# Second-set stores on ScalarE's DMA queue, and the prompt's output weights loaded 13 and used 15 steps later

## The chip, the cores and the metric

The kernel runs on one core of a Trainium2 chip. The metric is the device time of one execution in microseconds (us); less is better. The time before is 2841.52 us, the median of three runs (2840.78 to 2841.62).

The core's engines run side by side, each through its own list of instructions in order: TensorE (PE in the profile; PEld is its weight loads), VectorE (DVE), ScalarE (ACT), GpSimd (POOL), and SyncE (SP), which here only issues DMAs. DMAs can also be issued by ACT; in this kernel q1 is SP's hardware queue and q10 ACT's. An instruction at an engine's head that has to wait holds up all that stands behind it on that engine, and this holds for an issue of a DMA as for a computation.

## The reference

One inference step of two layers, on 256 prompt tokens and 2048 sample tokens (a grid of 32 rows by 64 columns), with a width of 1024 and 16 heads of 64. Layer 0 is a convolution branch, layer 1 neighbourhood attention. Each is `x = x + gate * Mixer(RMSNorm(x) * (1 + scale) + shift)`. Cut to what the change touches:

```python
q, k, v, z = na_project(h, w_in)                 # h @ w_in, 1024 -> 4 x 1024
# prompt tokens: softmax over the 256 prompt tokens
out = (context_attention(q, k, v) * silu(z)) @ w_out
# sample tokens: softmax over 8 x 16 neighbours on the grid and 512 cached context keys
att = neighbourhood_attention(q, k, v, cache_k, cache_v, rpb)
out = (att * silu(z)) @ w_out
x = x + gate * out
y = rms_norm(x, final_g)
```

All inputs and outputs are 32-bit floats. The kernel multiplies with full precision kept by splitting numbers into a rounded high part and the rest (`h` and `l` at the end of names), with three products per matmul of two split operands.

## The kernel before, in words

**First phase.** The convolution layer is followed by the projection into keys (part 1), queries (part 0), values and gates (part 3, `z`) of layer 1. Tokens go through it in two sets: the first has the prompt and the first 768 sample tokens, the second the sample tokens from 768 to 2047, in three blocks of 512, 512 and 256. For the second set, `na_rest` loops over 8 column tiles of 128 (two heads each), over the three parts, and over the three blocks: 24 matmuls into a PSUM bank, then an evacuation. A gate block is evacuated by ACT's Silu (L1005) and stored to the DRAM tensor `zn_d` (L1006); a key block is rounded by ACT (L1101), its rest made by POOL or DVE, and both parts are stored per head by `store_keys` (L1110, L1111) to `ks_d`; a query block is stored by `store_q` (L1076, L1082) to `qh_d` and `ql_d`. `store_keys` is also called by `context_keys`, for the cached keys (`kc_d`). The evacuated blocks are tiles of the pool tag `st` with 6 buffers, so a block's buffer comes free when its store is done. Beside the second set, woven in, run the context keys, the masked bias, the gated output weights (`w2_d`), the prompt's attention (which leaves its gated output in `yp_d`) and the context values. All these DMAs, loads and stores, are on SP's queue. In this phase of the second set a scheduler fixes the order on every engine.

**Second phase, `attention()`.** 256 units: 16 heads in two halves (`hg` 0 and 1), 4 groups `G` of 8 grid rows, 4 column blocks. A head here is one head in one row group, so 4 units. The order is half 0, groups 0 to 3 with 8 heads each, then half 1. In step i, PE's list has the transposes of unit i−2, the values of unit i−3 in every second step, and the scores of unit i+1 at the end. `load_head` asks for a head's keys, bias, queries (2 buffers), gates and values one head ahead. PE and DVE are ordered by hand in this phase; ACT, POOL and SP by the scheduler.

The output projection is done by `out_group` in side chunks of 6 matmuls, one in each step without values, and one more in every fourth step while more than 16 are due. `out_group` goes over 128-token row tiles and two halves `h` of 512 columns (12 matmuls each, L1644 to L1646), with the bank evacuated in a later step by ACT (`evacuate`, L1668) and added to the residual `x` by POOL (L1669). The residual tile is loaded (L1627) into one of 3 buffers. Its two weight tiles per half (a high and a low part, 1 MB each) come from `load_w2` (L1600), into 4 buffers, so that one pair (`hg`, `g`) fills them; `g` is 0 for the prompt and 1 for the sample. The next pair's half is asked for when the last row tile's matmuls of that half have been issued, in the order (0, 0), (1, 0), (0, 1), (1, 1). For the first pair, `W2_STEP` sets the step; there `hold` writes one element of each tile on DVE first (L1599), so that the DMA can't be issued before DVE is at that step.

`BEGIN` is the step in which both halves of the prompt are put into the list of side work (with the loads of `yp` and a pause of 3 chunks). Before a row group's first output tile is made, `split` forces side chunks until no more than 7 row tiles are open, the new ones with them; this is the case first in unit 45, where group 0's tiles have been queued and group 1's are to be made.

Names: `o0_None_1_0` is the prompt's tile of half `hg` 0, row tile 1, column half 0; `o0_0_0_0` that of sample group 0. `w2h010` is the high part of the weights of `hg` 0, `g` 1, column half 0. `a0_6_qh` are the queries of group 0, head 6; `sa1_3_1_S` the scores of group 1, head 3, column block 1.

Of the kernel before, what the change touches and what calls it, by code (L numbers as in the profile page):

```python
# [11 lines left out]
F32 = mybir.dt.float32  # L12
# [33 lines left out]
ADA_LAG = 3.5  # L46
LEAD = 1.9
TMP = 4
BEGIN = 10
WAIT = 3  # L50
NEAR = 3
W2_STEP = 5
START = 45.0

W_START = {1: (0.55, 25.8, 26.6), 0: (26.0, 38.6, 39.5), 2: (36.0, 52.0, 52.6)}
# [21 lines left out]
class Kern:  # L77
    def __init__(self, ctx, tc, io):
        self.tc, self.nc, self.io = tc, tc.nc, io
        self.ctx = ctx  # L80
        self.cp = ctx.enter_context(tc.tile_pool(name="consts", bufs=1))
        self.dr = ctx.enter_context(tc.tile_pool(name="scratch", bufs=1, space=bass.MemoryType.DRAM))
        d = lambda name, shape: self.dr.tile(shape, F32, name=name, tag=name)
        self.zc_d = d("zc_d", [D, NTOK])
        self.wl_d = d("wl_d", [3 * NK, P, D])
        self.vc_d = d("vc_d", [D, VCOLS])
        self.x1_d = d("x1_d", [NTOK, D])
        self.qh_d = d("qh_d", [D, NTOK])
        self.ql_d = d("ql_d", [D, NTOK])
        self.ks_d = d("ks_d", [NH, 2, DH, NTOK])  # L90
        self.vp_d = d("vp_d", [NPR, NH, 2, DH])
        self.vs_d = d("vs_d", [GW // CW, NSA // GW, CW, NH, 2, DH])
        self.bm_d = d("bm_d", [NH, 3, P, 3, 480])
        self.zn_d = d("zn_d", [D, NTOK])
        self.kc_d = d("kc_d", [NH, 2, DH, NCTX])
        self.cvs_d = d("cvs_d", [NCTX, NH, 2, DH])
        self.w2_d = d("w2_d", [2, 2, D, D])
        self.x2_d = d("x2_d", [NTOK, D])
        self.gate_d = d("gate_d", [2, 2, D])
        self.rpb_d = d("rpb_d", [P + 1, RPB_PITCH])  # L100
        self.yp_d = d("yp_d", [NK, 2, P, NPR])
# [224 lines left out]
    def weight(self, w, c0, name):  # L326

        nc = self.nc
        return self.halves(w[:, c0 : c0 + P].rearrange("(k p) n -> p k n", p=P), [P, NK, P], name)
# [649 lines left out]
    def na_rest(self, blocks):  # L979

        nc, io = self.nc, self.io
        w_in = io["na_w_in"][0]
        order = lambda ct: (3, 1, 0) if ct == NK - 1 else (1, 0, 3)
        todo = [(ct, part) for ct in range(NK) for part in order(ct)]
        weight = lambda ct, part: self.weight(w_in, part * D + ct * P, f"ni{blocks[0][0]}{blocks[0][1]}_{ct}_{part}")
        ahead = weight(*todo.pop(0))
        yield
        for ct in range(NK):
            rows = slice(ct * P, ct * P + P)
            for part in order(ct):  # L990
                w = ahead
                if todo:
                    ahead = weight(*todo.pop(0))
                for src, t0, n, hi, lo in blocks:
                    nm = f"ni_{ct}_{part}_{src}{t0}"
                    pm = self.mm_bank(nm)[:, :n]
                    self.project(pm, w, (hi, lo))
                    a = self.col(src, t0)
                    if part == 1:
                        self.keys(ct, src, t0, n, pm, nm)  # L1000
                        continue
                    f = self.st(F32, nm + "_f", [P, n])
                    if part == 3:
                        with self.tc.high_priority():
                            nc.scalar.activation(f, pm, AF.Silu)  # L1005
                        nc.sync.dma_start(self.zn_d[rows, a : a + n], f)  # L1006
                        continue
                    fo, po = f, pm
                    if src == "s":
                        fo = f.rearrange("p (j r c) -> p r j c", j=4, c=16)  # L1010
                        po = pm.rearrange("p (r j c) -> p r j c", j=4, c=16)
                    with self.tc.high_priority():
                        nc.scalar.activation(fo, po, AF.Copy, scale=-(DH ** -0.5))
                    fh, fl = (self.st(F32R, f"{nm}_{s}", [P, n]) for s in ("h", "l"))
                    self.round_pool(fh, f)
                    self.rest_pool(fl, f, fh)
                    self.store_q(self.qh_d, rows, src, t0, n, fh.bitcast(F32))
                    self.store_q(self.ql_d, rows, src, t0, n, fl.bitcast(F32))
                yield
# [46 lines left out]
    def windows(raw, at, R):  # L1066

        ap = raw[:, at : at + 1]
        return bass.AP(ap.tensor, ap.offset, [ap.ap[0], [CW, 4], [BIAS_COLS, R], [1, CW]])

    def store_q(self, dst, rows, src, t0, n, f):

        nc = self.nc
        a = self.col(src, t0)
        if src == "p" or n == 512:
            nc.sync.dma_start(dst[rows, a : a + n], f)  # L1076
            return
        g0 = self.col(src, t0 // 512 * 512)
        r0 = t0 % 512 // GW
        nr = n // GW  # L1080
        d = dst[rows, g0 : g0 + 512].rearrange("p (j r c) -> p j (r c)", j=4, c=16)[:, :, r0 * 16 : (r0 + nr) * 16]
        nc.sync.dma_start(d, f.rearrange("p (j x) -> p j x", j=4))  # L1082

    def keys(self, ct, src, t0, n, pm, nm):

# [20 lines left out]
    def store_keys(self, dst, ct, a, n, kh, kl):  # L1106
        for i in range(2):
            h = 2 * ct + i
            sl = slice(i * DH, i * DH + DH)
            self.nc.sync.dma_start(dst[h, i, :, a : a + n], kh[sl, :].bitcast(F32))  # L1110
            self.nc.sync.dma_start(dst[h, 1 - i, :, a : a + n], kl[sl, :].bitcast(F32))  # L1111

    def context_keys(self):
        nc, io = self.nc, self.io
# [150 lines left out]
    def phase1(self):  # L1265
        tc = self.tc
        with ExitStack() as c:
# [30 lines left out]
                pass  # L1298
            late.close()
            norms.close()  # L1300
            rest = self.na_rest(B)
            with tc.tile_pool(name="bp", bufs=1, side="right") as self.bp:
                with tc.tile_pool(name="mb", bufs=1, side="right") as self.mb:
# [57 lines left out]
    def attention(self):  # L1361
# [10 lines left out]
        for i in range(-1, len(units) + 4):  # L1372
            self.step = i
            if i == W2_STEP:
                for h in range(2):
                    self.load_w2(0, 0, h, True)
            if i == BEGIN:
                for hg in range(2):
# [375 lines left out]
```

## Time and profile before

| | |
|---|---|
| time, median of 3 runs | 2841.52 us |
| the profiled execution's own time | 2847.02 us |
| its span | 2845.2 us |
| mean granted clock of PE | 0.981 |
| HBM read, written | 359.86 MB, 189.22 MB |

The profile is of one execution, which took 5.5 us more than the median; 1.8 us of its time lie outside the span. Times in its views count from the span's start. The second set runs from about 1360 to 1840 us, the second phase from there to the end. Busy shares are of the span; an engine that waits is not busy, and issuing DMAs is not counted as busy either.

### The profile page before, as it was taken

The page shows a single profiled execution, that of the slowest core. Times are in us where ns is not written, and L with a number is a line of the kernel's source. Part 1 is how long each engine was busy: PE and PEld are TensorE (multiplying, and loading weights), DVE is VectorE, ACT ScalarE, POOL GpSimd, SP SyncE. Part 2 cuts the span into 40 slices and gives each one's busy share as a digit, 9 for nine tenths or more (in the row PEclk, how much of TensorE's full clock was granted, in tenths as well). Part 3 has the DMA queues.
Part 4 walks back from the last instruction along what each step waited for, and adds up shares of the span by engine and source line. Part 5 has one row for each costly group of instructions (what it writes and reads, how often), then busy time and mean ns, then how long its engine had stood idle before and what let it go on. Part 6 is the DMA issues. An engine that isn't in the chain of part 4 may idle for free. (4 is left out here: it accounts for less than half of the span.)

```text
span 2845.2 us, 45399 instructions
## 1 busy us (share of the span) xinstructions
PE 2702.7 (95%) x16079; PEld 2339.1 (82%) x16079; DVE 1848.0 (65%) x3126; ACT 1448.6 (51%) x2544; POOL 1507.1 (53%) x1631
## 2 busy tenths in 40 slices
PE   6999999999899999999989999879999999999998
PEld 4888877777677888999988888768888898888887
DVE  4789989999886510023455632157787787777885
ACT  4457565667544311234222244246676666666774
POOL 4679878889653343355113325235555555455563
PEclk9999999999899999999999999999999999999999
DMA  7233554555445554447789996688876787866763
GB/s 254 68 121 117 185 187 158 179 177 187 154 120 164 165 156 130 131 141 229 240 285 347 346 307 194 185 247 221 245 206 190 200 216 181 239 184 178 199 168 105
DMA packets 435627, 548.02 MB, mean 193 GB/s; under 512 B 42945, under 2 KB 306201, under 8 KB 435272
## 3 DMA queue, kind: packets, MB, share of 16 engines
q1 hardware_dynamic: 430080, 522.17, 61.3%
q10 hardware_dynamic: 5320, 22.95, 2.1%
q8 instruction: 128, 2.10, 0.3%
q14 instruction: 99, 0.81, 0.1%
HBM read 359.86 MB, written 189.22 MB: 193 GB/s over the span
## 5 line engine op out<-in xcount | busy, mean ns | idle before, releaser
L1508 POOL TENSOR_SCALAR sa_p<-sa_p,sa_m 128x992 f32<-128x992 f32 (+2 forms) x256 | 278.6, 1088 | 445.7 <-DVE sa_m L1507 321.7
L502 DVE SCALAR_TENSOR_TENSOR cv<-u,dw,cv 128x640 f32<-128x640 f32 (+2 forms) x570 | 427.9, 822 | 3.7 <-ACT cv L498 2.8
L1523 ACT CAST sa_pt<-sa_T 128x512 fp32r<-128x512 f32 (+3 forms) x512 | 275.2, 588 | 235.0 <-PE sa_T L1514 230.6
L111 DVE TENSOR_TENSOR sa_pt<-sa_T,sa_pt 128x512 fp32r<-128x512 f32 (+3 forms) x512 | 328.4, 682 | 3.2 <-ACT sa_pt L1523 3.0
L351 PE MATMUL ci_ps<-h_s_hi,ci_wh 128*128 128x512 f32 x768 | 307.5, 400 | 2.0 <-DVE shift L239 1.0
L353 PE MATMUL ci_ps<-h_s_hi,ci_wl 128*128 128x512 f32 x768 | 303.2, 395 | 0.0
L352 PE MATMUL ci_ps<-h_s_lo,ci_wh 128*128 128x512 f32 x768 | 302.9, 394 | 0.0
L1500 DVE TENSOR_REDUCE sa_m<-sa_S 128x1 f32<-128x512 f32 x256 | 176.2, 688 | 184.2 <-PE sa_S L1482 169.7
L1506 ACT ACTIVATE sa_p<-sa_S,sa_m 128x992 f32<-128x992 f32 (+2 forms) x256 | 267.3, 1044 | 53.7 <-DVE sa_m L1502 42.4
L1514 PE MATMUL sa_T<-ident,sa_p 128*128 128x128 f32 (+3 forms) x2048 | 271.6, 275 | 8.1 <-DVE sa_pt L111 7.3
L1514 PEld LDWEIGHTS sa_T<-ident,sa_p 128*128 128x128 f32 (+3 forms) x2048 | 238.5, 138 | 42.5 <-issue 12.0
L480 ACT ACTIVATE cv_p<-u,dw 128x640 f32<-128x640 f32 (+2 forms) x326 | 241.4, 770 | 55.4 <-POOL cv_s L483 37.7
L483 POOL TENSOR_TENSOR cv_s<-cv_s,cv_p 128x519 f32<-128x519 f32 (+1 forms) x155 | 233.1, 1504 | 68.3 <-DVE cv_s L506 45.5
L483 POOL TENSOR_TENSOR cv_p<-cv_p,cv_p 128x520 f32<-128x520 f32 (+1 forms) x155 | 227.7, 1469 | 27.1 <-ACT cv_p L480 19.5
L1543 PE MATMUL sa_O<-sa_pt,a_v 120*128 120x256 f32 (+5 forms) x1280 | 192.5, 281 | 0.0
L1538 PE MATMUL sa_O<-sa_pt,cv 128*128 128x256 f32 x1024 | 176.3, 295 | 4.2 <-DVE 1_0_of L1557 1.7
L351 PEld LDWEIGHTS ci_ps<-h_s_hi,ci_wh 128*128 128x128 f32 x768 | 145.5, 189 | 39.3 <-ACT cv_p L480 2.5
L1502 DVE CUSTOM_DVE_ANT_0 sa_S<-sa_S,a_bm,sa_m 128x480 f32<-128x480 f32 (+2 forms) x256 | 170.9, 668 | 9.1
L353 PEld LDWEIGHTS ci_ps<-h_s_hi,ci_wl 128*128 128x128 f32 x768 | 145.1, 189 | 33.8
L352 PEld LDWEIGHTS ci_ps<-h_s_lo,ci_wh 128*128 128x128 f32 x768 | 145.6, 190 | 30.9
L1543 PEld LDWEIGHTS sa_O<-sa_pt,a_v 120*128 120x128 f32 (+2 forms) x1280 | 169.1, 193 | 0.0
L351 PE MATMUL ni_s<-h_s_hi,nis_wh 128*128 128x512 f32 x384 | 152.2, 396 | 12.4 <-DVE ni_s_l L111 8.7
(843 smaller groups left out, 7198.6 us busy)
## 6 DMA issues: line engine op xcount, KB each, us to landing
adaw<-in_ada_w SPq DMA_DIRECT2D x24, 1024.0 KB
ci_w<-in_conv_w_in SPq DMA_DIRECT2D x48, 512.0 KB
a_bm<-bm_d SPq DMA_DIRECT2D x32, 720.0 KB
x_s<-in_x_sample SPq DMA_DIRECT2D x32, 512.0 KB
vs_d<-v_s SPq DMA_DIRECT2D x128, 128.0 KB
a_qh<-qh_d SPq DMA_DIRECT2D x128, 128.0 KB
a_ql<-ql_d SPq DMA_DIRECT2D x128, 128.0 KB
o_x<-x_d SPq DMA_DIRECT2D x32, 512.0 KB
```

The source lines that it names most:

```text
L111: self.nc.vector.tensor_tensor(out=lo, in0=src, in1=hi.bitcast(F32), op=ALU.subtract)
L351: self.nc.tensor.matmul(out, wh[:, k, :], hh[:, k, :], start=k == 0, stop=False)
L352: self.nc.tensor.matmul(out, wh[:, k, :], hl[:, k, :], start=False, stop=False)
L353: self.nc.tensor.matmul(out, wl[:, k, :], hh[:, k, :], start=False, stop=k == NK - 1)
L480: nc.scalar.activation(t, st["u"][:, c0 + tap : c1 + tap], AF.Copy, scale=self.dw[:, ct, tap : tap + 1])
L483: nc.gpsimd.tensor_tensor(out=st["sum", half], in0=st["sum", half], in1=st[half, tap], op=ALU.add)
L502: nc.vector.scalar_tensor_tensor(out=out, in0=u, scalar=w, in1=first, op0=ALU.mult, op1=ALU.add)
L1506: nc.scalar.activation(p[:, n], S[:, n], AF.Exp, scale=-1.0, bias=m[:, 2:3], accum_out=m[:, 3:4])
L1508: nc.gpsimd.tensor_scalar(out=p[:, n], in0=p[:, n], scalar1=m[:, 3:4], scalar2=1.0, op0=ALU.mult, op1=ALU.mult)
L1514: nc.tensor.transpose(t[:w, c * P : c * P + P], p[:, x + c * w : x + c * w + w], self.ident)
L1523: nc.scalar.copy(pt[:w, 0, part, :, at], t)
L1543: nc.tensor.matmul(dst, v[:w, c0 + c].rearrange("p s d -> p (s d)"), loc[:, lo:hi], start=False, stop=s == 1 and c == 3)
```

## The change

Two numbers are raised: `BEGIN` from 10 to 25, and `W2_STEP` from 5 to 18. A flag `second` is set ahead of the second set's `na_rest`, and a helper `store` issues on ACT's queue while it is set, on SP's otherwise. The gate stores, `store_q` and `store_keys` go through it. That moves 200 DMAs to ACT's queue: 24 of gates, 48 of queries, 96 of keys and 32 of the cached keys. The stores of values, bias, gated weights and the prompt's attention stay on SP, as all loads do. Behind the flag lines count one to six more than before (L1005 is L1006, L1482 is L1488, L1600 is L1606, L1644 is L1650); the moved stores all have L1074.

```diff
@@ -46,10 +46,10 @@
 ADA_LAG = 3.5
 LEAD = 1.9
 TMP = 4
-BEGIN = 10
+BEGIN = 25
 WAIT = 3
 NEAR = 3
-W2_STEP = 5
+W2_STEP = 18
 START = 45.0
 
 W_START = {1: (0.55, 25.8, 26.6), 0: (26.0, 38.6, 39.5), 2: (36.0, 52.0, 52.6)}
@@ -78,6 +78,7 @@
     def __init__(self, ctx, tc, io):
         self.tc, self.nc, self.io = tc, tc.nc, io
         self.ctx = ctx
+        self.second = False
         self.cp = ctx.enter_context(tc.tile_pool(name="consts", bufs=1))
         self.dr = ctx.enter_context(tc.tile_pool(name="scratch", bufs=1, space=bass.MemoryType.DRAM))
         d = lambda name, shape: self.dr.tile(shape, F32, name=name, tag=name)
@@ -1003,7 +1004,7 @@
                     if part == 3:
                         with self.tc.high_priority():
                             nc.scalar.activation(f, pm, AF.Silu)
-                        nc.sync.dma_start(self.zn_d[rows, a : a + n], f)
+                        self.store(self.zn_d[rows, a : a + n], f)
                         continue
                     fo, po = f, pm
                     if src == "s":
@@ -1068,18 +1069,22 @@
         ap = raw[:, at : at + 1]
         return bass.AP(ap.tensor, ap.offset, [ap.ap[0], [CW, 4], [BIAS_COLS, R], [1, CW]])
 
+    def store(self, dst, src):
+
+        (self.nc.scalar if self.second else self.nc.sync).dma_start(dst, src)
+
     def store_q(self, dst, rows, src, t0, n, f):
 
         nc = self.nc
         a = self.col(src, t0)
         if src == "p" or n == 512:
-            nc.sync.dma_start(dst[rows, a : a + n], f)
+            self.store(dst[rows, a : a + n], f)
             return
         g0 = self.col(src, t0 // 512 * 512)
         r0 = t0 % 512 // GW
         nr = n // GW
         d = dst[rows, g0 : g0 + 512].rearrange("p (j r c) -> p j (r c)", j=4, c=16)[:, :, r0 * 16 : (r0 + nr) * 16]
-        nc.sync.dma_start(d, f.rearrange("p (j x) -> p j x", j=4))
+        self.store(d, f.rearrange("p (j x) -> p j x", j=4))
 
     def keys(self, ct, src, t0, n, pm, nm):
 
@@ -1107,8 +1112,8 @@
         for i in range(2):
             h = 2 * ct + i
             sl = slice(i * DH, i * DH + DH)
-            self.nc.sync.dma_start(dst[h, i, :, a : a + n], kh[sl, :].bitcast(F32))
-            self.nc.sync.dma_start(dst[h, 1 - i, :, a : a + n], kl[sl, :].bitcast(F32))
+            self.store(dst[h, i, :, a : a + n], kh[sl, :].bitcast(F32))
+            self.store(dst[h, 1 - i, :, a : a + n], kl[sl, :].bitcast(F32))
 
     def context_keys(self):
         nc, io = self.nc, self.io
@@ -1298,6 +1303,7 @@
                 pass
             late.close()
             norms.close()
+            self.second = True
             rest = self.na_rest(B)
             with tc.tile_pool(name="bp", bufs=1, side="right") as self.bp:
                 with tc.tile_pool(name="mb", bufs=1, side="right") as self.mb:
```

How it moves instructions is shown at three places. First, ACT's list at the end of the second set (the gates of a column tile, `ni_3`, and then its keys, `ni_1`; `pa` is the prompt's attention). Before:

```order
L1231 COPY pa_t<-pa_O 64x256
L1005 ACTIVATE ni_3_s_f<-ni_3_s_16991 128x512
L1005 ACTIVATE ni_3_s_f<-ni_3_s_17019 128x256
L1101 CAST ni_1_s_h<-ni_1_s_17053 128x512
L1101 CAST ni_1_s_h<-ni_1_s_17086 128x512
```

After:

```order
L1236 COPY pa_t<-pa_O 64x256
L1074 DMA zn_d<-ni_3_s_f 128x512
L1006 ACTIVATE ni_3_s_f<-ni_3_s_16991 128x512
L1074 DMA zn_d<-ni_3_s_f 128x512
L1006 ACTIVATE ni_3_s_f<-ni_3_s_17019 128x256
L1074 DMA zn_d<-ni_3_s_f 128x256
L1106 CAST ni_1_s_h<-ni_1_s_17053 128x512
L1074 DMA ks_d<-ni_1_s_h 64x512
L1074 DMA ks_d<-ni_1_s_l 64x512
```

The numbers in `ni_3` and `ni_1` are the parts. Each gate's store stands behind its Silu on ACT, and the store of a key's low part, which ACT doesn't make, stands ahead of ACT's next evacuation.

Second, SP's list around the prompt's first weights. Before:

```order
L1467 DMA ck7_18307<-kc_d_71 128x512
L1600 DMA w2h000_17397<-w2_d_73 128x4x512
L1600 DMA w2l000_17398<-w2_d_73 128x4x512
L1600 DMA w2h001_17403<-w2_d_73 128x4x512
L1600 DMA w2l001_17404<-w2_d_73 128x4x512
L1469 DMA cv7_18309<-cvs_d_72 128x4x128
L1477 DMA a0_3_v_17516<-vs_d_68 88x8x128
L1454 DMA a0_3_qh_17519<-qh_d_64 64x512
L1445 DMA a0_3_k_17514<-ks_d_66 128x704
```

After:

```order
L1460 DMA a0_5_ql_17853<-ql_d_65 64x512 x2
L1623 DMA yp0_1h_18292<-yp_d_77 128x4x128
L1623 DMA yp0_1l_18293<-yp_d_77 128x4x128
L1623 DMA yp1_0h_19039<-yp_d_77 128x4x128
L1623 DMA yp1_0l_19040<-yp_d_77 128x4x128
L1606 DMA w2h000_17944<-w2_d_73 128x4x512
L1606 DMA w2l000_17945<-w2_d_73 128x4x512
L1606 DMA w2h001_17950<-w2_d_73 128x4x512
L1606 DMA w2l001_17951<-w2_d_73 128x4x512
L1483 DMA a0_6_v_18027<-vs_d_68 88x8x128
L1460 DMA a0_6_qh_18030<-qh_d_64 64x512
L1451 DMA a0_6_k_18025<-ks_d_66 128x704
```

The four tiles stood ahead of head 3's loads, and stand ahead of head 6's, with four loads of `yp` ahead of them.

Third, PE's list in unit 45, where the matmuls that `split` forces reach the sample's first tile. Before:

```order
L1482 MATMUL sa1_3_1_S_19274<-a1_3_k_19030,a1_3_ql_19036 128x480
L1514 MATMUL sa1_2_3_T0_19279<-ident_98,sa1_2_3_p_19205 128x128 x4
L1514 MATMUL sa1_2_3_T1_19284<-ident_98,sa1_2_3_p_19205 120x128 x4
L1644 MATMUL o0_0_0_0_19304<-w2h010_18937,0_1_y0h_17811 128x512
L1645 MATMUL o0_0_0_0_19304<-w2l010_18938,0_1_y0h_17811 128x512
```

After:

```order
L1650 MATMUL o1_None_1_1_19266<-w2h101_19004,yp1_1h_19041 128x512
L1651 MATMUL o1_None_1_1_19266<-w2l101_19005,yp1_1h_19041 128x512
L1652 MATMUL o1_None_1_1_19266<-w2h101_19004,yp1_1l_19042 128x512
L1650 MATMUL o0_0_0_0_19290<-w2h010_19259,0_1_y0h_17749 128x512
L1651 MATMUL o0_0_0_0_19290<-w2l010_19260,0_1_y0h_17749 128x512
```

The prompt's second half stood in side chunks spread over the steps 27 to 40, and its four tiles now stand in unit 45, right ahead of the sample's first tile. That tile's weights, `w2h010` and `w2l010`, take the buffers which the prompt's second half reads. From unit 46 on, PE's list is the same in both.

## The prediction

> **What bounds the kernel now.** I read the page's busy times first, then windows to find the stages in which TensorE (PE) is not full, then PE's waits and the chain of waits in those.
>
> ```profile
> PE 2702.7 (95%) x16079; PEld 2339.1 (82%) x16079; DVE 1848.0 (65%) x3126; ACT 1448.6 (51%) x2544; POOL 1507.1 (53%) x1631
> q1 hardware_dynamic: 430080, 522.17, 61.3%
> q10 hardware_dynamic: 5320, 22.95, 2.1%
> ```
>
> PE is busy for 95% of 2845.2 us and nothing else is above 65%, so time is lost only where PE stands still or its granted clock falls. SP's queue is q1 with 522 MB, ACT's is q10 with 23 MB. The windows (us, PE, PEld, DVE, ACT, POOL, granted clock, DMA share, GB/s) show where:
>
> ```profile
> 1360.00:1520.00 160.00, 144.21 (x1016) 134.65 (x1015) 81.31 (x126) 36.58 (x68) 31.88 (x17) 0.97 0.84 273
> 1520.00:1800.00 280.00, 280.00 (x1547) 244.49 (x1546) 122.24 (x190) 100.29 (x207) 105.28 (x102) 1.00 0.84 279
> 1827.00:1831.00 4.00, 3.92 (x10) 3.16 (x11) 0.03 (x1) 0.60 (x1) 1.90 (x2) 0.56 0.58 145
> 1843.00:1873.00 30.00, 28.42 (x192) 24.74 (x192) 25.91 (x65) 21.76 (x41) 10.90 (x11) 0.94 1.05 338
> 1864.00:1873.00 9.00, 9.00 (x72) 8.59 (x70) 7.74 (x19) 6.17 (x13) 3.08 (x4) 1.00 1.04 385
> 1878.00:1891.00 13.00, 3.65 (x13) 2.98 (x14) 1.34 (x3) 0.59 (x1) 2.93 (x9) 0.51 1.03 207
> 1942.00:1948.00 6.00, 5.87 (x32) 5.66 (x33) 2.74 (x6) 2.14 (x4) 0.99 (x1) 0.72 1.05 244
> 1968.00:1978.00 10.00, 10.00 (x67) 8.94 (x66) 8.25 (x18) 6.42 (x12) 2.69 (x3) 1.00 0.83 225
> ```
>
> The second set begins at 1360 with 15.8 us of standing still, then PE is full from 1520 to 1800; the attention's start, behind that, stands repeatedly, and after each stand the clock is near half for some us. PE's waits from 1800 to 2035 (total, times, longest), and the chain there (start, us):
>
> ```profile
> PE sa_S L1481 <- DMA a_qh<-qh_d: 11.3, 1, 11.3
> PE sa_S L1482 <- DMA a_ql<-ql_d: 8.2, 4, 3.6
> PE ni_s L351 <- DVE ni_s_l L111: 7.1, 1, 7.1
> PE o_None L1644 <- ACT o_None_o L1668: 1.4, 2, 0.7
> ...
> 1818.51 7.53 DMA zn_d<-ni_s_f
> 1826.14 0.38 ACT ni_s_h L1101
> 1826.60 0.44 DVE ni_s_l L111
> 1827.08 0.80 PE ni_s L351
> 1861.77 15.76 DMA w2l<-w_d
> 1877.57 10.41 DMA a_ql<-ql_d
> 1888.11 0.77 PE sa_S L1482
> ```
>
> Two causes stand there. A gate store sits late on SP's queue, and the key evacuation behind it needs its buffer. And four 1 MB tiles of the prompt's output weights go ahead of a head's queries.
>
> **What it removes.**
>
> ```profile
> 1798.00 0.60 ACT L1005 ACTIVATE ni_s_f<-ni_s 128x512 f32<-128x512 f32 x1 [4.48 <-PE ni_s L353]
> 1884.52 0.76 PE L1481 MATMUL sa_S<-ck,a_qh 128*128 128x512 f32 x1 [11.29 <-DMA a_qh<-qh_d]
> ```
>
> (a) The gates were ready at 1798.6 and their store was issued at 1818.51: 19.9 us in SP's line. On ACT's queue it is issued at once and, with the same 7.53 in flight, lands near 1806, before PE needs the buffer at 1820. The 7.1 us wait goes, and the clock behind it (4 us at 0.56, so 1.8): **−8.9**.
> (b) W2(0,0) leaves the place ahead of head 3's loads. The 11.29 us stand goes, and the 2.8 behind it for the second query tile (from 1885.28 to 1888.11), and half clock over 3.65 us of work (1.8): **−15.9**.
> (c) Of the 8.2 us for ql tiles, 2.8 are already in (b). The other 5.4, at heads 5 and 6, come where out_group's loads crowd the queue; side work now starts 15 steps later, so I take them off with their clock (6 us at 0.72, 1.7): **−7.1**.
> The evacuation waits of o_None (1.4) recur, they are neither gained nor lost. Sum removed: 31.9.
>
> **What it adds.** The hold copies stood in step 5:
>
> ```profile
> L1599 DVE CAST w2h<-mhalf x2: 132/138/143, 1853.7 to 1853.8; 128x1 fp32r<-128x1 f32 x2
> 1843.28 0.99 POOL L1508 TENSOR_SCALAR sa_p<-sa_p,sa_m 128x864 f32<-128x864 f32 x1 [4.13 <-issue]
> ...
> 1871.66 0.99 POOL L1508 TENSOR_SCALAR sa_p<-sa_p,sa_m 128x864 f32<-128x864 f32 x1 [1.67 <-PE sa_O L1543]
> ```
>
> Ten steps without side work lie between the last two rows: 2.84 us each. From the hold at 1853.7 to the scores of head 3's first unit (1884.52 − 11.29 = 1873.23) are 19.5 us.
>
> (e) The hold at step 18 stands ahead of head 6, one step nearer: 16.7 us. A head is 1.79 MB of small pieces, at 207 to 225 GB/s (windows 1878 and 1968) 8.3 us. At the hold a backlog stands: head 5's 8.3, a gate tile 0.7 and four yp tiles 2.7 (1.31 MB at 385), 1.5 taken for flight, less three steps of 2.84 since head 5's buffers came free, so 4.7. Then W2's 4.19 MB at 385 GB/s (window 1864), 10.9, and head 6's 8.3: 23.9 against 16.7. PE stands 7.2 us, with clock 2.0: **+9.2**. Bounds: 0 if the backlog is gone and the queue runs at 385 throughout, 16 if it goes as at head 3 (b).
> (f) W2(1,0) now comes between steps 39 and 44, four tiles in five steps; 10.9 us of load against five steps of 2.84: **0**, up to 5 (half of the load) if a head's loads fall on it.
> (g) At unit 45 the split forces the prompt's last four tiles (48 matmuls) and two of the sample in a row, and W2(0,1) is used right behind the tiles whose buffers it needs. Twelve matmuls fill a tile's half:
>
> ```profile
> 1923.47 0.40 PE L1645 MATMUL o_None<-w2l,yp_1h 128*128 128x512 f32 x1
> 1924.61 0.40 PE L1481 MATMUL sa_S<-ck,a_qh 128*128 128x512 f32 x1
> ...
> 1797.80 0.28 PE L351 MATMUL ni_s<-h_s_hl,nis_wh 128*128 128x256 f32 x1
> 1800.62 0.39 PE L351 MATMUL ni_s<-h_s_hi,nis_wh 128*128 128x512 f32 x1
> ```
>
> Five of them lie between the first two starts, so 0.228 each and 2.74 for twelve (the 24 of 256 columns of a second-set group, between the last two, take 2.82). The first half (2.10 MB, 5.45 us at 385, 1.0 for flight) is asked for 2.74 before the burst's end: it lands 3.7 behind it, 0.7 of which an evacuation wait takes already (row o_None). The second half lands 5.45 later, while 12 matmuls and 0.7 pass: 2.1 more. 5.1, with clock 1.7: **+6.8**. Bounds 3 (the first half alone) and 17.5 (the 15.76 us that the last W2 tile took in the chain, with clock 1.7).
> (h) The residual x of o_0_1 waits for a prompt row's store, and its add now stands ahead of a POOL normalisation:
>
> ```profile
> SPq L1627 <- DMA x_d<-o_None_x: 5.2, 1, 5.2
> ```
>
> Nothing to 5.2; I take **+2**: nothing of PE's waits for x itself, only POOL's normalisation behind the add could.
> (i) Fifteen more steps have no side work to fill PE's short gaps; in the ten units without any (window 1843) PE stood 1.6 of 30 us, or 0.15 a unit, part of it at the start. I take 0.1 a step, **+1.5**, between 0 and 3. Sum added: 19.5.
>
> **The second set's line.** All 200 moved stores (30.4 MB) lie between 1360 and 1840.
>
> ```profile
> PE v_ps_s L973 <- DVE v_s L111: 6.5, 5, 2.3
> ACT v_s L1038 <- DMA vs_d<-v_s: 8.2, 4, 4.8
> ...
> L1110 SPq DMA_DIRECT2D kc_d<-ck_h x16: 484/580/1634, 1371.7 to 1399.6; - x16
> L1674 ACTq DMA_DIRECT2D x_d<-o_x x16: 326/326/333, 2031.8 to 2461.3; - x16
> ```
>
> The first two rows are waits from 1360 to 1520: value evacuations wait for their own stores, vs_d, which stay on SP but stood there behind 32 kc_d stores of 0.58 us each (18.6 us of issuing). These leave; the loads behind gain too. PE's 15.8 us there and 3% of clock (4.8) could at most go, 20.6; but DMA share is 0.84 already, so I take **−2.5**, near nothing, between −20 and +24. What is added is ACT's issuing: 200 × 0.33 to 0.58, 66 to 116 us in 480. ACT is busy 36% of 1520–1800, so it has room on average. A store also waits on ACT for what it stores. The low part is made by POOL after ACT, and what stands behind it on ACT is the next PSUM evacuation, which PE waits for two groups later:
>
> ```profile
> 1828.83 1.28 POOL L108 TENSOR_TENSOR ni_s_l<-ni_s_f,ni_s_h 128x512 fp32r<-128x512 f32 x1
> ```
>
> 1.28 and two issues (0.7) are 2.0, under the 2.82 us of a 256-column group, so it is hidden as long as POOL is on time; the cover gone, it is the slower rival below.
>
> **A rule against it.** The Trainium skill, "DMA: Bandwidth & Descriptors", section "Issuing engines are not separate DMA queues", says that DMAs of every issuer run on the same 16 engines and interleave, and that several issuers save only the sequencer's time, usually small. By it (a) would be nothing and the sum −6.0. The row 1818.51 speaks against it here: the store's flight was 7.53 us, its standing in line 19.9.
>
> **Sum.** −31.9 + 19.5 − 2.5 = **−14.9**. On the profiled execution's own time of 2847.02 that is 2832.1; this execution is 5.5 above the median 2841.52, and the difference taken from the median gives 2826.6, so 2827.
>
> **Rivals.**
> R1, the weights take their full price: term (g) is 17.5 instead of 6.8, −4.2 in all, 2837.3. For it: in the chain the last W2 tile took 15.76 us with heads beside it. Against: behind unit 45 fewer head loads stand in line. Chance 0.20.
> R2, the slower side: ACT's queue holds up evacuations where PE is full (1520–1800). It decides once POOL's low part comes over 0.8 us late (2.82 − 2.0). Price: about 1 us (a POOL normalisation or rest beside it is 0.99 to 1.28) for 3 blocks in 8 column tiles, 24. Then +9.1, 2850.6. For it: POOL has 105 us of side work there, unsplit. Against: 62% of POOL is free. Chance 0.17.
> R3, the stores land no sooner, because what they lack is the engines: (a) is gone, −6.0, 2835.5. For it: DMA share 0.84 around. Against: 19.9 against 7.53. Chance 0.05.
> R4, the second set's stands go by 15.8 instead of 2.5: −28.2, 2813.3. For it: its waits are for stores in SP's line; against: 273 GB/s is moved there, and the loads themselves remain. Chance 0.13.
> The forecast as it stands has 0.45.
>
> **How the numbers follow.** A measurement tells about 0.2% (5.7 us) from no change. Faster: forecast, R4 and most of R3, 0.61. Same: R1 and the rest, 0.22. Slower: R2, 0.17. For 8 in 10 the range goes from below R4 (with bounds of (e) and (c) the other way) at 2808 up to 2848, short of R2 at its full price.
>
> **What would show it.** After: ACT's queue near 53 MB; no 7 us wait of PE for ni_s's low part at 1820; head 3 on time and a wait of about 7 us for a_qh or a_ql at head 6; a PE wait of 3 and one of 2 us for w2h or w2l at unit 45; PE still full between 1520 and 1800. Wrong would be PE waits for ACT's evacuations there (R2), or a wait of over 10 us for the weights (R1); or a growth of the 15.8 us between 1360 and 1520 (the −2.5).

## The result and the profile after

The changed kernel takes 2854.08 us (median of 4 runs, 2851.91 to 2856.84), the one before 2841.15 us: a ratio of 1.0046, with a 95% interval of 1.0031 to 1.0060. 13 us are lost where 14.9 of gain were forecast, and the time lies outside the range.

The page of the changed kernel, its busy times and queues:

```profile
PE 2699.5 (95%) x16079; PEld 2332.0 (82%) x16079; DVE 1842.9 (65%) x3126; ACT 1448.3 (51%) x2544; POOL 1506.5 (53%) x1631
q1 hardware_dynamic: 403328, 491.75, 57.8%
q10 hardware_dynamic: 32072, 53.37, 5.5%
```

The 30.4 MB did move to ACT's queue, and no engine does more work. The windows (us, PE, PEld, DVE, ACT, POOL, granted clock, DMA share, GB/s):

```profile
1360.00:1520.00 160.00, 133.55 (x945) 125.44 (x946) 80.34 (x134) 33.77 (x64) 31.61 (x16) 0.95 0.88 283
1520.00:1800.00 280.00, 279.39 (x1541) 243.62 (x1540) 117.19 (x179) 101.87 (x207) 102.64 (x101) 1.00 0.81 267
```

From 1360 to 1520 PE is busy for 133.6 us; it was 144.2 before. Behind 1520 it is nearly full, as before. PE's waits there, and behind 1820 (total, times, longest):

```profile
PE v_ps_s L974 <- DVE v_s L112: 15.1, 11, 3.0
PE ni_s L352 <- DVE ni_s_l L112: 11.0, 1, 11.0
...
PE sa_S L1487 <- DMA a_qh<-qh_d: 5.8, 1, 5.8
PE sa_T L1520 <- DVE sa_pt L112: 5.0, 10, 1.5
PE ni_s L352 <- DVE ni_s_l L112: 3.8, 1, 3.8
PE sa_S L1488 <- DMA a_ql<-ql_d: 3.6, 2, 3.3
PE o L1650 <- DMA w2h<-w_d: 2.6, 1, 2.6
PE o L1651 <- DMA w2l<-w_d: 1.8, 1, 1.8
```

The second part is near the forecast: head 6's wait in place of head 3's, two waits for weights at unit 45. The first is not: the waits for the values' low parts have more than doubled, a stand of 11 us for a key block is new, and of the 7.1 us behind 1820, 3.8 are still there. From 1360 to 1520 PE's waits sum up to 26.5 us; they were 15.8. What held the key block stands in ACT's timeline (start, us, what, and the idle time before with its releaser):

```profile
1477.88 0.59 ACT L1106 CAST ni_s_h<-ni_s 128x512 fp32r<-128x512 f32 x1 [4.25 <-PE ni_s L354]
1481.31 0.62 ACT L1166 CAST w_100h<-w_100t 128x512 fp32r<-128x512 f32 x1 [2.83 <-DVE w_100t L1165]
1490.87 1.63 ACTq L1074 DMA_DIRECT2D ks_d<-ni_s_h  x2
1494.20 2.09 ACTq L1074 DMA_DIRECT2D ks_d<-ni_s_l  x2
1496.39 0.59 ACT L1106 CAST ni_s_h<-ni_s 128x512 fp32r<-128x512 f32 x1 [14.46 <-DMA bm_d<-bm]
```

ACT made the key's high part by 1478.47, and issued its store at 1490.87. Nothing of that store was missing: the tile was ready, and ACT had nothing else to do from 1481.93 on. ACT's next work, a key evacuation behind four stores, came after 14.46 us of idling. The row names a bias store (`bm_d`) as the releaser; that is the profile's inference, and this bias store landed only at 1497.95. The evacuation started 0.1 us behind the issue of the last of the four stores: it waited for the stores, and the question is what they waited for.

The built program shows why. It has eight completion counters (semaphores that a landing DMA increments) for the DMAs of SP and ACT together, given out in turn; in the trace, too, every DMA of the two counts on one of the same eight. Each DMA's issue waits until the DMA that had its counter last has landed, so at most eight are under way, and the line is one for both queues. ACT's list with its waits, there (DMAHW0 to DMAHW7 are the counters):

```
L1106 CAST ni_0_1_s1024_h_13812<-ni_0_1_s1024_13787 128x512 [waits DMAHW0_49,DMAHW7_49,PE_49,Activation_49]
L1166 CAST w2_100h_15586<-w2_100t_15585 128x512 [waits DMAHW6_49,DVE_49]
L1074 DMA ks_d_66<-ni_0_1_s1024_h_13812 64x512 [waits DMAHW6_49,Activation_49]
L1074 DMA ks_d_66<-ni_0_1_s1024_h_13812 64x512 [waits DMAHW0_49]
L1074 DMA ks_d_66<-ni_0_1_s1024_l_13813 64x512 [waits DMAHW2_49,DVE_49]
```

The second store reads what the first does and waits for a counter alone (DMAHW0). The trace has each counter's increments. The four stores stood 8.9, 0.7, 1.7 and 1.2 us, 12.5 of the 14.46, and each stand ended within 0.1 us of the last increment of the store's own counter, which had been given last to a DMA of SP: for the first, a bias store that SP had issued at 1485.15.

Over all 200 moved stores, 70 stood for over 0.3 us on ACT, 96.3 us in all. 44 of these (68.3 us) ended within 0.2 us of the last increment of the store's own counter, and for 35 (60.9 us) the DMA counted there was one of SP's. The other 26 (28.0 us) are not told apart here; low parts that come late are among the possible reasons. Not each of them costs PE time: 34.5 of the 96.3 us lie between 1543 and 1810, where PE stood 0.6 us in all.

### The profile page after: what moved, and what is told of

The parts are those of the page before. It is cut to its first block, busy times and chain, and to the rows that moved or that the text cites. A ratio compares the mean times of both kernels' runs of the same rounds, so it can differ in the third digit from the quotient of the medians.

```text
span 2850.1 us, 45331 instructions
## 1 busy us (share of the span) xinstructions
PE 2699.5 (95%) x16079; PEld 2332.0 (82%) x16079; DVE 1842.9 (65%) x3126; ACT 1448.3 (51%) x2544; POOL 1506.5 (53%) x1631
## 5 line engine op out<-in xcount | busy, mean ns | idle before, releaser
L484 POOL TENSOR_TENSOR cv_p<-cv_p,cv_p 128x520 f32<-128x520 f32 (+1 forms) x155 | 227.7, 1469 | 26.5 <-ACT cv_p L481 18.8
L109 POOL TENSOR_TENSOR nis_wl<-nis_w,nis_wh 128x1024 fp32r<-128x1024 f32 x24 | 58.8, 2454 | 227.5 <-ACT nis_wh L344 177.8
L352 PE MATMUL ni_s<-h_s_hi,nis_wh 128*128 128x512 f32 x384 | 152.0, 396 | 15.8 <-DVE ni_s_l L112 15.4
```

Of the source, the lines that this page charges most:

```text
L352: self.nc.tensor.matmul(out, wh[:, k, :], hh[:, k, :], start=k == 0, stop=False)
L484: nc.gpsimd.tensor_tensor(out=st["sum", half], in0=st["sum", half], in1=st[half, tap], op=ALU.add)
```

## The experiments

In the traces I compare the second set by three stretches of PE: A from the prompt's last value matmul to the second set's first `ni_s` matmul, B from there to the 301st, C to the 1701st (of 1728). Their bounds are starts in the timelines; in C, 290.1 is what the kernels without the wait at 1820 take. "Set" goes on to the first scores.

| kernel | A | B | C | set | ratio to before (95%) |
|---|---|---|---|---|---|
| before | 151.8 | 66.3 | 299.1 | 521.7 | |
| changed | 158.4 | 71.2 | 296.6 | 531.2 | 1.0046 (1.0031 to 1.0060) |
| e1_stores | 160.3 | 69.1 | 297.0 | 531.0 | 1.0052 (1.0039 to 1.0065) |
| e2_steps | 151.5 | 65.1 | 299.3 | 520.3 | 1.0006 (0.9996 to 1.0015) |
| e3_gates | 151.3 | 72.4 | 290.1 | 518.1 | 1.0013 (1.0000 to 1.0025) |
| e4_no_context | 150.1 | 74.7 | 301.3 | 530.5 | 1.0029 (1.0019 to 1.0039) |
| e5_pool | 167.0 | 69.9 | 293.8 | 535.1 | 1.0071 (1.0048 to 1.0095) |
| e7_last_gates | 150.9 | 65.5 | 290.1 | 510.9 | 0.9987 (0.9973 to 1.0001) |
| e9_extra | 155.2 | 61.2 | 300.4 | 521.3 | 1.0005 (0.9993 to 1.0016) |
| e10_pool_rest | 154.3 | 76.4 | 290.9 | 526.1 | 1.0029 (1.0018 to 1.0039) |
| e16_late_gates | 153.7 | 65.0 | 290.1 | 515.4 | 0.9991 (0.9979 to 1.0002) |

Each line's stretches are of one execution, while the ratios are of all; A varied by some us where nothing in it was changed (150.9 in e7, 153.7 in e16), so single us there mean little.

**The two parts apart.** e1_stores sets `BEGIN = 10` and `W2_STEP = 5` again; e2_steps has the new steps, with

```diff
-            self.second = True
+            self.second = False
```

> Only the stores are moved to ACT's queue; the two steps are as before. Theory S (in the second set, ACT's evacuations now stand behind stores that wait, and PE waits for them): slower than before by 5 to 15 us, with PE waits for the low parts of values and keys between 1360 and 1520 of over 20 us (15.8 before). Theory W (the change is slow because of the burst of side work in unit 45 and the weights' loads): within 3 us of before or up to 10 faster, since the wait for the gate store goes.

> Only the two steps are changed; all stores stay on SP's queue. Theory S: between 5 us faster and 4 us slower than before; the stand at head 3 goes and comes back as waits at head 6, unit 45 and behind it. Theory W: slower than before by 8 us or more.

The stores alone give the whole loss, 2853.23 against 2839.26 us; the steps alone give nothing that can be measured, 2840.25. Theory S holds, W falls. Of e1's 14.0 us the table's one execution shows 9.3 in the set; where the rest lies is open. e1's waits of PE from 1360 to 1520 are those of the changed kernel again:

```profile
PE v_ps_s L974 <- DVE v_s L112: 14.5, 8, 3.3
PE ni_s L352 <- DVE ni_s_l L112: 9.3, 1, 9.3
```

**Which stores.** In e3_gates the gates alone are moved; in e4_no_context all but the cached keys:

```diff
-            self.store(dst[h, i, :, a : a + n], kh[sl, :].bitcast(F32))
-            self.store(dst[h, 1 - i, :, a : a + n], kl[sl, :].bitcast(F32))
+            q = self.store if dst is self.ks_d else self.nc.sync.dma_start
+            q(dst[h, i, :, a : a + n], kh[sl, :].bitcast(F32))
+            q(dst[h, 1 - i, :, a : a + n], kl[sl, :].bitcast(F32))
```

> Only the 24 gate stores of the second set go out on ACT's queue, steps as before. If standing in SP's line was what delayed the gate store, as the prediction's step (a) has it: 5 to 9 us faster, and no PE wait at 1820. If a store on ACT's queue has to wait for the same earlier DMAs anyway (the build has each DMA issue wait for the landing of the one eight before it, whichever queue that is on): within 4 us of before, the wait at 1820 being partly there.

> Stores of gates, queries and keys on ACT's queue, the cached keys' 32 stores on SP's, steps as before. If the cached keys' stores are what delays the value evacuations on ACT (PE waits of 15.1 us for them in the changed kernel, 6.5 before): 5 to 9 us faster than the kernel that moves all stores. If key and query stores are what costs: within 3 us of that kernel.

e4 is some 6 us faster than e1 (8.3 over before against 14.0), as expected if the cached keys' stores delay the value evacuations. Its A is back at 150, and PE's waits for the values' low parts from 1360 to 1520 are 5.8 us (6.5 before, 14.5 in e1): these stores, issued by ACT between value evacuations, cost stretch A 6.6 us in the changed kernel and 8.5 in e1, less what A varies by. The rest is in B and C.

e3 fits neither expectation as a whole: the wait at 1820 is gone, as by the first, but the kernel is no faster (1.0013; 2843.58 against 2839.26 us in the medians). It is the clearest case, since its lists of the engines stay nearly as before but for the 24 stores. C gains 9.0 us: that is the wait at 1820 with its clock, gone as forecast. B loses 6.0. There the timelines of ACT and PE have:

```profile
1505.97 0.60 ACT L1006 ACTIVATE ni_s_f<-ni_s 128x512 f32<-128x512 f32 x1 [5.71 <-POOL ni_s_l L109]
1513.54 0.35 ACTq L1007 DMA_DIRECT2D zn_d<-ni_s_f  x1
1514.01 0.62 ACT L1166 CAST w_200h<-w_200t 128x512 fp32r<-128x512 f32 x1 [7.44 <-DMA qh_d<-ni_s_h]
1514.54 0.59 ACT L1006 ACTIVATE ni_s_f<-ni_s 128x512 f32<-128x512 f32 x1
...
1506.77 0.45 SPq L336 DMA_DIRECT2D nis_w<-in_na_w_in  x1
...
1515.18 0.80 PE L352 MATMUL ni_s<-h_s_hi,nis_wh 128*128 128x512 f32 x1 [4.88 <-ACT ni_s_f L1006]
```

A gate was ready at 1506.57, its store waited until 1513.54, and the next evacuation stood behind it; PE stood 4.88 us for that. The store's counter had been given last to the load in SP's row, 512 KB of weights; its 16 increments came from 1511.95 to 1513.46. The set is 3.6 us shorter all the same, so what e3 loses against before comes behind it; the two traces put 3.8 us there, and the rest is open.

**ACT's time or ACT's waits?** e9_extra keeps all stores on SP and gives ACT other work in their place:

```diff
+            self.extra(kh, kl)
...
+    def extra(self, *tiles):
+        if self.second:
+            for t in tiles:
+                self.nc.scalar.copy(self.scr, t[:, :256])
```

> All stores on SP and the steps as before; 178 copies of 128x256 (0.37 us each, 66 us in all) are added on ACT in the second set, each reading the tile that a store reads and writing a tile that nobody reads. They take ACT's time and wait for what the stores would wait for on ACT, but for no DMA. Theory L: within 4 us of before. Theory I (ACT's time for issuing, or its wait for POOL's and DVE's low parts, is what delays the evacuations): 8 us slower or more.

2844.55 us, a ratio of 1.0005 with 1 in its interval. In the trace ACT is busy for 64 us more than before (1512.8 against 1448.6) and stands 43 us ahead of the copies, nearly all of it for parts that POOL and DVE make, and this costs nothing that can be measured. Theory I falls; what costs is what a store waits for besides.

**A queue with other counters.** e5_pool issues the 200 stores on GpSimd, whose DMAs count on eight other semaphores in the trace; e10_pool_rest does it without the cached keys.

```diff
-        (self.nc.scalar if self.second else self.nc.sync).dma_start(dst, src)
+        (self.nc.gpsimd if self.second else self.nc.sync).dma_start(dst, src)
```

> The 200 stores go out on GpSimd's queue instead of ACT's, steps as before. Theory L (the issue of a DMA on SP's or ACT's queue waits for the landing of the DMA eight before it on either; on ACT these waits stand ahead of PSUM evacuations): GpSimd's stores have counters of their own and ACT is free, so this is at least 6 us faster than the kernel with all stores on ACT, and PE's waits from 1360 to 1520 are near the 15.8 us of before or less. Theory D (the 16 DMA engines are full, any second queue only shifts the wait): within 4 us of the kernel with all stores on ACT. Open for both: GpSimd's own work can be late behind the stores.

> Stores of gates, queries and keys of the second set on GpSimd's queue, the cached keys' on SP's, steps as before; the kernel with the same stores on ACT's queue was 8 us slower than before. Theory L (ACT stands ahead of its stores until an SP DMA on the same completion counter has landed, and the evacuations behind it are late): GpSimd's DMAs have other counters, ACT issues nothing, so the loss goes: between 8 us faster than before and 3 slower. Theory D (the engines are full and a second queue shifts the landing of what PE needs): 6 us or more slower than before, as on ACT's queue.

Both whole times missed theory L's expectation: e5 is 20 us slower than before, with 24.9 us of PE's waits from 1360 to 1520, and e10, 8.8 us slower, is as slow as e4. Theory D's expectation missed in e5 (6 us slower than e1, where at most 4 were expected) and was met in e10. The stretches tell more. In C, where e4's ACT stood for its stores, e10 takes 290.9 against 301.3 us: without the shared counters these 10 us are gone, as L has it. In B e10 takes 76.4, the most of all, though ACT issues nothing. There ACT's timeline shows other waits:

```profile
1490.42 0.62 ACT L1167 CAST w_101h<-w_101t 128x512 fp32r<-128x512 f32 x1 [6.30 <-DMA w_d<-w_011t]
1490.95 0.36 ACT L1106 CAST ni_s_h<-ni_s 128x256 fp32r<-128x256 f32 x1
1499.24 1.05 ACT L344 CAST nis_wh<-nis_w 128x1024 fp32r<-128x1024 f32 x1 [7.93 <-DMA nis_w<-in_na_w_in]
...
1521.65 0.62 ACT L1167 CAST w_200h<-w_200t 128x512 fp32r<-128x512 f32 x1 [8.51 <-DVE w_200t L1166]
1522.18 0.59 ACT L1006 ACTIVATE ni_s_f<-ni_s 128x512 f32<-128x512 f32 x1
```

The casts at 1490 and 1521 are side work, the gated output weights; their inputs come late, and an evacuation stands behind each. In e10's list these casts stand earlier: the last of them behind 39 of the second set's 72 `ni` evacuations on ACT, in the kernel before behind 43. So with the stores off SP the scheduler has moved side work forward. The cast at 1499 waited for a load of the projection's own weights on SP's queue (5.26 us for such a load in the kernel before), and this is what theory D would give. Which of the two costs e10 its B is not shown; no run takes either away. Shown is that ACT's stands cost B where the order is nearly the same (e3); how much of the loss in B of e1 and e4 is order or full engines stays open. A of e5 (167.0) with the cached keys on GpSimd stays open too; a value evacuation there waits up to 11.0 us for its own store on SP.

**The gate stores where the line is short.** The same 24 stores of e3, but only those of column tile 7 (e7_last_gates), or of tiles 2 to 7 (e16_late_gates), on ACT:

```diff
-(nc.scalar if self.second else nc.sync).dma_start(self.zn_d[rows, a : a + n], f)
+(nc.scalar if self.second and ct == NK - 1 else nc.sync).dma_start(self.zn_d[rows, a : a + n], f)
```

> Only the three gate stores of the last column tile go out on ACT's queue (all 24 did in the run before), steps as before. If the gain of the prediction's step (a) is real and was given back where the other gate stores stood on ACT between 1505 and 1525: 4 to 9 us faster than before, the wait at 1820 gone. If not: within 3 us of before.

> Gate stores of the column tiles 2 to 7 of the second set on ACT's queue, those of tiles 0 and 1 on SP's, steps as before. Theory L: ACT stood for gate stores between 1505 and 1525 only because SP's line of bias and gated-weight DMAs, with which it shares the completion counters, is long there; left out of that place, the loss goes and the gain at 1820 stays: 2 to 8 us faster than before, ACT's stands ahead of these stores under 7 us in all (14.0 with all 24). If gate stores on ACT's queue cost wherever they stand: no faster than before.

In both, B is back at 65 and C stays at 290.1. ACT stood ahead of its moved stores for 14.0 us in e3, 6.9 in e16 and 0 in e7. So B's loss goes with the stands, as L says; e16's 6.9 us fall in C, where they cost nothing. But the whole times fell short of what L expected of both: e7's set is 10.8 us shorter than before's and the kernel 2.6 us (0.9987, not clear of 1), e16's 6.3 and 1.6. e7's trace shows where it went:

```profile
PE sa_S L1487 <- DMA a_qh<-qh_d: 13.8, 1, 13.8
PE sa_S L1488 <- DMA a_ql<-ql_d: 12.4, 4, 4.6
```

These two rows were 11.3 and 8.2 before. The attention starts 10.8 us earlier, its loads do not come as much earlier, and at unit 46 it leads by 3.7.

**The steps, otherwise.** e8_apart keeps all stores on SP and asks for the prompt's first weights half by half:

```diff
-BEGIN = 25
-W2_STEP = 18
+BEGIN = 15
+W2_STEP = (7, 14)
...
-            if i == W2_STEP:
-                for h in range(2):
-                    self.load_w2(0, 0, h, True)
+            if i in W2_STEP:
+                self.load_w2(0, 0, W2_STEP.index(i), True)
```

> All stores on SP. The prompt's first weights are asked for half by half, the first at step 7 and the second at step 14, and the prompt's side work begins at step 15. If the loads' length ahead of one head is what makes PE stand (7.8 us at head 6 with four tiles together): halves of 5.4 us leave 0 to 3 us at each of two heads, and the whole is 4 to 12 us faster than before. If the queue has no room for them at all at this place: within 3 us of before.

2837.04 us, 0.9984 (0.9970 to 0.9998): 4 us faster than before, at the low end. Together with e7's three stores:

> The two changes of earlier runs together: the last column tile's three gate stores on ACT's queue, and the prompt's first weights asked for in two halves at steps 7 and 14, the side work from step 15. If the time that the gate stores save is taken back where the heads' loads are waited for, and the halves remove that wait: 7 to 13 us faster than before. If the two do not add: 2 to 6 us faster.

2836.61 us, 4.0 us faster than before, 0.9984 (0.9972 to 0.9997): the two do not add.

**Fewer and bigger stores.** If the line moves by landings, merging stores should shorten it. e13_merge makes the four stores of a key block two; e14_low merges only the low part's two; e15_all is e11 with e14's merge.

```diff
+        hs = dst.rearrange("h s d t -> (h s) d t")
+        self.nc.sync.dma_start(hs[4 * ct : 4 * ct + 4 : 3, :, a : a + n], kh.bitcast(F32))
+        rows = dst.rearrange("h s d t -> (h s d) t")
+        r = (4 * ct + 1) * DH
+        self.nc.sync.dma_start(rows[r : r + P, a : a + n], kl.bitcast(F32))
```

> All stores on SP, steps as before; the four stores of each key block and of each block of cached keys are made two, of 128 partitions each, with the same bytes. If SP's line moves by landings, one for one (theory L: a DMA is issued when the one eight before it has landed), twice the bytes behind a counter shorten the line: 3 to 10 us faster than before, and a shorter wait for the gate store at 1820. If the line moves at the rate of the 16 engines: within 3 us of before.

> All stores on SP, steps as before; of the four stores of a key block only the two of the low part are made one, of 128 partitions with one stride, which can go to all 16 engines (the merged high part, with two blocks of rows, counted up its counter 3 times instead of 16 and took 10.4 us to land instead of 3.5). If SP's line moves by landings, one DMA for one eight before it: 2 to 8 us faster. If it moves at the engines' rate: within 3 us of before. If the merged store lands late too: slower by 5 us or more.

> The last column tile's gate stores on ACT's queue, the prompt's weights in two halves at steps 7 and 14 with the side work from step 15, and the low parts' stores merged. If the merged store helps: 6 to 13 us faster than before. If it does nothing: 4 to 5 us faster, as without it. If it lands late: no faster than before.

e13 takes 2910.41 us, 70 more than before, and neither theory had that (see the end). e14 takes 2845.15, 1.0014 (1.0004 to 1.0024), 3.7 us slower, between its expectations: no gain, so the line doesn't go faster with fewer DMAs; this part of theory L, that only the count of DMAs sets the line's pace, falls. e15, 2835.64 and 0.9984 (0.9973 to 0.9995), is no better than e8 alone. These three, e8, e11 and e15, are the only versions that are faster than the kernel before and clear of no change, by 0.16%.

## Why the prediction was wrong, point by point

- **(a), the gate store: right by itself, undone by the key stores.** The gain in C was sized rightly: 9.0 us in e3, e7 and e16 against 8.9. At this place "on ACT's queue it is issued at once" held in the changed kernel, too:

```profile
1807.93 0.60 ACT L1006 ACTIVATE ni_s_f<-ni_s 128x512 f32<-128x512 f32 x1 [4.48 <-PE ni_s L354]
1808.56 0.33 ACTq L1074 DMA_DIRECT2D zn_d<-ni_s_f  x1
...
1817.52 0.46 ACTq L1074 DMA_DIRECT2D ks_d<-ni_s_h  x1
1822.40 0.45 ACTq L1074 DMA_DIRECT2D ks_d<-ni_s_l  x1
1825.38 0.45 ACTq L1074 DMA_DIRECT2D ks_d<-ni_s_h  x1
1826.28 0.45 ACTq L1074 DMA_DIRECT2D ks_d<-ni_s_l  x1
1826.83 0.59 ACT L1106 CAST ni_s_h<-ni_s 128x512 fp32r<-128x512 f32 x1 [10.04 <-DMA a_z<-zn_d]
```

The gate store went out 0.03 us behind its Silu. What failed is "the 7.1 us wait goes": the key stores that were moved with it stood on ACT, the second one 4.42 us, until loads of the attention on SP's queue with the same counters had landed, and the next key evacuation stood behind them. PE still waited 3.8 us, and C gained 2.5 us instead of 9.0. (In stretch B gate stores stood as well, one for 6.96 us in e3.)
- **The second set's line: where it failed most.** −2.5 was taken. A grew by 6.6 and B by 4.9 in the changed kernel, +11.4. The bound of +24 held it, and the sign that it named came: PE's 15.8 us of waits from 1360 to 1520 became 26.5. The step that failed is the price of a store on ACT: its issuing time, 0.33 to 0.58 us, and a wait for POOL's low part. The wait for a landing, on a counter that SP's DMAs share, was put at nothing. ACT stood 18.3 us for the cached keys' stores between A's value evacuations, and 24.5 us for moved stores in B. Sum for the set: −11.4 forecast, +9.5 in the profiles (531.2 − 521.7). That is 20.9 of the 27.8 us between forecast and measurement.
- **R2** had the right sign and the right victim, evacuations behind a waiting store on ACT, at +9.1 and a chance of 0.17. Its mechanism (POOL's low part) and its place (1520 to 1800, where PE stayed full) were both wrong: e9 has those waits and loses nothing. That its price came near is luck. R1, R3 and R4 fell: the waits for weights at unit 45 stayed at 4.4 us, the gate store did land sooner where it was moved alone (e3), and the set's stands grew. A list of the waits that each store carries, read before the prediction, shows the counter.
- **(b)** held: the 11.3 us at head 3 and the 2.8 behind them are gone in e2. **(c)** held for the waits: those of heads 5 and 6 are gone, and what e2 has for a_ql at head 6 belongs to (e). **(e)** was too small: 7.2 forecast at head 6; e2's trace has 7.5 us for a_qh there and 2.5 for a_ql behind it, the changed kernel's 5.8 and 3.3. **(g)**: 3.0 and 2.1 forecast at unit 45 (the working gives 2.0 for the second); 2.6 and 1.8 came. **(h)**: 2 forecast, 2.7 lost between the scores of units 46 and 55.
- **(i)** came near. e2's rows for PE's waits from unit 12 on show it:

```profile
PE sa_S L1487 <- DMA a_qh<-qh_d: 7.5, 1, 7.5
PE sa_T L1520 <- DVE sa_pt L112: 4.3, 7, 1.5
PE sa_S L1488 <- DMA a_ql<-ql_d: 2.5, 1, 2.5
```

Waiting for DVE's `sa_pt` cost 0.9 us from unit 12 on before, and 4.3 in e2; but 1.5 of these stand in unit 50 and are part of (h)'s 2.7. Ahead of unit 46 it is 1.9 more, 1.5 forecast. All steps from (b) to (i) together were to give −3.5; by e2's runs they give +1.0 (0.9996 to 1.0015, that is −1 to +4), a small miss beside the set's; (e), 2.8 us too small by e2's trace, is the largest part of it that the traces show.
- **The Trainium skill's rule** ("DMA: Bandwidth & Descriptors", "Issuing engines are not separate DMA queues") was set aside on the row of 19.9 us in line. For C that was right, 9.0 us were to be had. Its first half says that both issuers share what carries the DMAs; in this program they share the counters too, and then a second issuer can cost, 14 us here (e1).

## What to carry to other kernels

Before a store is moved to a computing engine's queue, list what its issue waits for in the built program, the reuse of completion counters among it: that engine then stands until an unrelated transfer lands, with its evacuations behind. Such stands cost where an evacuation behind them ends a wait of the bounding engine (stretch B), and next to nothing where there is slack (1543 to 1810). Here only the gate stores outside B ended a wait without such a loss, and even their gain at the end isn't clear of nothing. A wait that is removed ahead of a stage that waits for its loads can come back there: 10.8 us won ahead of the attention in e7's trace were 3.7 by unit 46, and 2.6 in the medians.

## What the runs showed of the hardware that was not expected

A store of 128 partitions whose destination has two blocks of 64 rows as its outermost dimension (e13's high part) moved its counter in 3 increments instead of 16 (median of 21) and took 10.4 us to land; the stores of 64 rows that it replaced took 3.5 (median of 48). The merged low part of the same run, with its 16 increments, took 9.9 (median of 21), so the other stores were late beside it. From 1400 to 1480 the DMA share fell to 0.65 (0.81 before) and PE's busy time to 53.5 us (73.9 before):

```profile
1400.00:1480.00 80.00, 53.49 (x352) 51.64 (x351) 31.70 (x50) 13.58 (x26) 10.03 (x4) 0.83 0.65 213
```

The Trainium skill, "DMA: Bandwidth & Descriptors", "Why a DMA increments its semaphore by 16 and not by 1", says that the outermost dimension's size limits how many of the 16 engines carry a DMA, two here; the few increments agree: one comes about 1 us after the issue, and two within 0.7 us of each other at the end. In e14, where the high parts are not merged, the merged low part, 128 rows with one stride, had its 16 increments and took 4.0 us. So the merged high part is what made e13 slow; that it did so by crowding two engines is not shown.
